# A feed-forward network's gate and up products, 17 of 22 blocks by one level of Strassen's algorithm

## Chip, core and metric

One core of a Trainium2 chip runs one program. The metric is the device time of one execution in microseconds (us), here the median of several runs. TensorE (PE in the profile) multiplies, VectorE (DVE) and ScalarE (ACT) work element by element, GpSimd is POOL, and SyncE (SP) issues the transfers.

## What is computed

One residual block on 512 tokens of width 1024: a token mixer (windowed attention beside gated linear attention), a cross attention to 256 memory tokens, a SwiGLU network, a last RMS norm. The change lies in the network and in the norms at its two ends:

```python
def _rms(t, w):
    y = t * lax.rsqrt(jnp.mean(t * t, axis=-1, keepdims=True) + EPS)
    return y * w

def _swiglu(h, w_gate, w_up, w_down):
    return (jax.nn.silu(h @ w_gate) * (h @ w_up)) @ w_down

x += _swiglu(_rms(x, w_ffn), w_gate, w_up, w_down)   # 1024 -> 2816 -> 1024
out = _rms(x, w_out)
```

## The kernel before

Tokens lie along the free axis, so a tile holds 128 features by 512 tokens; the residual stream is 8 such tiles, `res`. Every float32 product is made of three: an operand x is split by `split` (L97, L98) into a rounded high part on ACT (`H`, `ah`, `xh`) and a low part x - high on DVE (`L`, `al`, `xl`), and `prod3` gives high x high, high x low and low x high. `unit` loads a tile of weights (512 KB, by SP's queue) and splits it; its tags R, H and L have three buffers each. `block` runs the matmuls of one output tile, three for each 128 rows of the inner dimension, into a bank of PSUM. `ps_mm` has four banks that are used in turn, `ps_s` some others, `ps_t` one.

The network is the last part. `weighted` makes `zh`, `zl`, the two parts of the stream times the norm's weight; the factor of each token (1/rms, `n2.b`, spread over all partitions) is applied later. A loop over the 22 tiles of the hidden layer then runs a gate pass and an up pass of 24 matmuls 128x512 each, and behind them a chain per tile: L1022 gate times `n2.b` (DVE), SiLU (ACT, L93), L1024 times up, L1025 times `n2.b` (DVE), and a split into `ah[j]`, `al_[j]` that are kept for all 22 tiles. The squares, the sums and the reciprocal root of that norm (`Norm.add`, `Norm.finish`, `rsqrt` of nine small DVE operations) run beside the first passes. Calling the passes in order p0 (gate of tile 0), p1 (up of tile 0), p2 and so on, pass p4 writes the bank of p0.

Then come the down products: for each of 8 output tiles 66 matmuls 128x512 and one addition to `res` (L1040). The last output is made in two halves of the tokens, 66 matmuls 128x256 each. After each half the last norm is finished (L199 squares, sums on PE with a matrix of ones into `ps_t`, L216 to L178 on DVE, a spread over the partitions on PE with the identity into the same `ps_t`, L228), and `res` times this factor goes out: L1052 and L1058 on DVE, reading the spread from PSUM, L1056 on POOL, L1060 the transfer.

The order of an engine's instructions is set by a scheduler from the order of the code and a table of durations; the changed kernel writes parts of it out by hand.

Of the kernel before, what the change touches and what calls it, by code (L numbers as in the profile page):

```python
# [32 lines left out]


def build(tc, a, out):
    nc = tc.nc
    ctx = ExitStack()

    def pool(name, bufs=1, side=None, space=None):
        kw = {"name": name, "bufs": bufs, "reuse_waits": "tile"}  # L40
        if side is not None:
            kw["side"] = side
        if space is not None:
            kw["space"] = space
# [30 lines left out]
    def t2k(bufs=3):  # L75
        return tp.tile([P, 512], F32, tag="t2k", bufs=bufs, name=uniq("t2k"))
# [4 lines left out]
    def f(ap):  # L81
        return ap.bitcast(F32)
# [97 lines left out]
    class Norm:  # L180
# [23 lines left out]
            else:  # L204
                nc.vector.tensor_tensor(out=acc, in0=acc, in1=sq, op=ALU.add)

        def finish(self, spread=True, cols=None):
# [7 lines left out]
            v = cp.tile([P, nt], F32, name=uniq(f"v_{self.name}"))  # L215
            nc.vector.tensor_scalar(  # L216
                out=v, in0=ps[:, 0 : 2 * nt].rearrange("p (t c) -> p t c", c=2)[:, :, 0],
                scalar1=1.0 / D, scalar2=EPS, op0=ALU.mult, op1=ALU.add,
            )
# [89 lines left out]
    r0 = sp.tile([P, S], F32, tag="sm", bufs=4, name="r0")[:, 0:P]  # L309
    h0, l0 = (sp.tile([P, S], F32R, tag="q", bufs=8, name=n)[:, 0:P] for n in ("h0", "l0"))  # L310
# [16 lines left out]
    for u in range(1, KC // 2):  # L327
# [24 lines left out]
    wf_w = small("wf_w", [P, KC], a["norm_ffn_w"])  # L352
# [304 lines left out]
    for pr in range(2):  # L657
        qh, ql = [], []
        for h in (2 * pr, 2 * pr + 1):
            pq = ps_mm()  # L660
# [22 lines left out]
        for t in range(NT):  # L683
            kh = gp.tile([P, 2, 256], F32R, tag="kh", bufs=2, name=uniq("kh"))
            kl = kls[t % 2]
            for c in range(2):
# [26 lines left out]
            for e in range(2):  # L713
                ts = slice(t * P, (t + 1) * P)
# [295 lines left out]
    ah = [fp.tile([P, S], F32R, name=f"ah{j}") for j in range(NF)]  # L1010
    al_ = [fp.tile([P, S], F32R, name=f"al{j}") for j in range(NF)]
    for j in range(NF):
        pg = ps_mm()
        block(pg, [(unit(a["w_fg"][j]), KC)], zh, zl)
        pu = ps_mm()
        block(pu, [(unit(a["w_fu"][j]), KC)], zh, zl)
        if j == 0:
            for i in range(KC):
                n2.add(res[i])
            n2.finish()  # L1020
        t = t2k()
        nc.vector.tensor_tensor(out=t, in0=pg, in1=n2.b, op=ALU.mult)  # L1022
        table_act(t, t, AF.Silu)
        nc.vector.tensor_tensor(out=t, in0=t, in1=pu, op=ALU.mult)  # L1024
        nc.vector.tensor_tensor(out=t, in0=t, in1=n2.b, op=ALU.mult)  # L1025
        split(ah[j], al_[j], t)

    n3 = Norm("n3", S)
    for j in range(KC):
        units = []  # L1030
        for k0 in range(0, NF, KC):
            nk_ = min(KC, NF - k0)
            units.append((unit(a["w_fd"][j][:, k0 * P : (k0 + nk_) * P]), nk_))
# [100 lines left out]
```

## Time and profile before

| | |
|---|---|
| median of 3 runs | 918.81 us (918.31 to 920.23) |
| the profiled execution: own time, and its span | 919.91 us, 918.1 us |
| mean granted TensorE clock | 0.995 of full speed |
| PE / PE weight load / DVE / ACT / POOL busy | 98 / 81 / 61 / 46 / 1% |
| matmuls | 4318 |
| the network's loop and down products | about 546 to 906 us of the span |
| from the last matmul 128x256 to the span's end | 905.87 to 918.1 us |

The span is what the hardware profiler saw between the first and the last instruction; the own time of the same execution has some 1.8 us around it. A share of busy time is an average over all stages; what bounds a stage is read from what its engines wait for. Matmuls overlap, so their pace is the distance between two starts, not the listed length.

### The profile page before, as it was taken

What the parts mean: (1) busy time and instruction counts of PE and PEld (TensorE: products, weight loads), DVE (VectorE), ACT (ScalarE), POOL (GpSimd) and SP (SyncE); (2) the same over time, 40 slices, a digit from 0 to 9 for tenths busy, and PEclk for the clock granted to TensorE, in tenths of its full rate; (3) what the DMA queues carried; (4) which work ended last, traced back from release to release, by engine and by line L of the source; (5) the groups of instructions that cost most, each with busy time, mean ns of one, the idle gap of its engine ahead of it and who ended that gap; (6) DMA issues with size and microseconds to landing.
All of it is one profiled execution on the core that took longest, in us unless ns stands there. A gap on an engine that the chain in (4) does not pass through costs nothing.

```text
span 918.1 us, 11424 instructions
## 1 busy us (share of the span) xinstructions
PE 901.2 (98%) x4318; PEld 746.7 (81%) x4318; DVE 557.4 (61%) x1104; ACT 426.5 (46%) x760; POOL 7.0 (1%) x30
## 2 busy tenths in 40 slices
PE   8999999999999999999999999999999999999995
PEld 6898888887888787778888778888888888888885
DVE  6777888777343959966766996444444444323323
ACT  7576574556333838463445864223332233222220
POOL 1000000000000000000000000000000000000001
PEclk9999999999999999999999999999999999999998
DMA  7232221222232031425432222232222322323212
GB/s 249 92 115 70 69 70 69 70 69 69 92 96 89 23 115 48 143 86 161 114 115 92 70 89 95 94 107 99 92 92 92 106 100 86 104 86 103 87 41 92
DMA packets 29415, 86.11 MB, mean 94 GB/s; under 512 B 4048, under 2 KB 7760, under 8 KB 29360
## 3 DMA queue, kind: packets, MB, share of 16 engines
q1 hardware_dynamic: 29216, 85.37, 28.9%
q8 instruction: 34, 0.56, 0.2%
q14 instruction: 21, 0.17, 0.1%
q10 hardware_dynamic: 144, 0.00, 0.0%
HBM read 83.27 MB, written 2.10 MB: 93 GB/s over the span
## 4 chain that ended last, share of the span: by engine, by line
PE 89%; DVE 6%; ACT 3%; DMA 1%; issue 1%; SPq 0%; DVEq 0%; ACTq 0%
PE mm L79 80%; PE s L79 3%; PE o L79 3%; PE t L79 1%; DVE L L98 1%; PE t L545 1%; ACT pm L93 1%; DMA R<-in_w_tg 1%; PE mm L545 1%; ACT H L97 1%; DVE sl L98 1%; DVE on L747 1%; DMA x<-in_xT 0%; PE t L758 0%; DVE st L706 0%
## 5 line engine op out<-in xcount | busy, mean ns | idle before, releaser
L97 ACT CAST H<-R 128x1024 fp32r<-128x1024 f32 (+2 forms) x155 | 156.8, 1013 | 326.1 <-PE mm L79 247.0
L98 DVE TENSOR_TENSOR L<-R,H 128x1024 fp32r<-128x1024 f32 (+2 forms) x155 | 181.8, 1174 | 93.9 <-ACT H L97 93.5
L79 PE MATMUL mm<-xl,H 128*128 128x512 f32 x592 | 232.3, 392 | 0.0
L79 PE MATMUL mm<-xh,L 128*128 128x512 f32 x592 | 232.1, 392 | 0.0
L79 PE MATMUL mm<-xh,H 128*128 128x512 f32 x592 | 230.6, 390 | 0.0
L79 PEld LDWEIGHTS mm<-xh,H 128*128 128x128 f32 x592 | 111.2, 188 | 22.5
L79 PEld LDWEIGHTS mm<-xl,H 128*128 128x128 f32 x592 | 111.2, 188 | 22.1
L79 PEld LDWEIGHTS mm<-xh,L 128*128 128x128 f32 x592 | 111.3, 188 | 21.7
L79 PE MATMUL mm<-ah,H 128*128 128x512 f32 (+1 forms) x198 | 72.5, 366 | 0.0
L79 PE MATMUL mm<-ah,L 128*128 128x512 f32 (+1 forms) x198 | 72.4, 366 | 0.0
L79 PE MATMUL mm<-al,H 128*128 128x512 f32 (+1 forms) x198 | 72.4, 365 | 0.0
L79 PE MATMUL mm<-H,xh 128*128 128x512 f32 (+1 forms) x192 | 70.3, 367 | 0.0
L79 PE MATMUL mm<-L,xh 128*128 128x512 f32 (+1 forms) x192 | 70.3, 366 | 0.0
L79 PE MATMUL mm<-H,xl 128*128 128x512 f32 (+1 forms) x192 | 70.1, 365 | 0.0
L1024 DVE TENSOR_TENSOR t2k<-t2k,mm 128x512 f32<-128x512 f32 x22 | 15.0, 687 | 68.3 <-PE mm L79 67.7
L93 ACT ACTIVATE p<-sm,nm,sc 128x256 f32<-128x256 f32 (+1 forms) x64 | 36.3, 569 | 25.4 <-DVE es L519 20.3
L1022 DVE TENSOR_TENSOR t2k<-mm,rb_n 128x512 f32<-128x512 f32 x22 | 15.1, 691 | 44.9 <-PE mm L79 43.0
L79 PEld LDWEIGHTS mm<-al,H 128*128 128x128 f32 x198 | 37.3, 189 | 6.1
L79 PEld LDWEIGHTS mm<-ah,H 128*128 128x128 f32 x198 | 37.3, 189 | 6.0
L79 PEld LDWEIGHTS mm<-ah,L 128*128 128x128 f32 x198 | 37.3, 189 | 6.0
L79 PEld LDWEIGHTS mm<-L,xh 128*128 128x128 f32 x192 | 36.1, 188 | 5.5 <-DVE L L98 0.6
L79 PEld LDWEIGHTS mm<-H,xh 128*128 128x128 f32 x192 | 36.3, 189 | 5.1 <-issue 0.2
(300 smaller groups left out, 1365.7 us busy)
## 6 DMA issues: line engine op xcount, KB each, us to landing
R<-in_w_fg SPq DMA_DIRECT2D x22, 512.0 KB, 3.2
R<-in_w_fu SPq DMA_DIRECT2D x22, 512.0 KB, 3.3
R<-in_w_gate SPq DMA_DIRECT2D x16, 512.0 KB, 3.3
R<-in_w_fd SPq DMA_DIRECT2D x16, 512.0 KB, 3.5
x<-in_xT SPq DMA_DIRECT2D x16, 256.0 KB, 3.5
R<-in_w_q SPq DMA_DIRECT2D x8, 512.0 KB, 3.5
R<-in_w_attn_o SPq DMA_DIRECT2D x8, 512.0 KB, 3.3
R<-in_w_vg SPq DMA_DIRECT2D x8, 512.0 KB, 3.3
```

Source lines behind the costliest of these rows:

```text
L79: nc.tensor.matmul(o, lhsT=lhsT, rhs=rhs, start=start, stop=stop)
L93: last_table[0] = nc.scalar.activation(*args, **kw)
L97: nc.scalar.copy(out=hi, in_=src)
L98: nc.vector.tensor_tensor(out=lo, in0=src, in1=f(hi), op=ALU.subtract)
L545: nc.tensor.transpose(out=pt[:, i * P : (i + 1) * P], in_=prs[i // 2][:, i % 2, b * P : (b + 1) * P], identity=ident)
L747: nc.vector.scalar_tensor_tensor(out=on[t][:, vs], in0=on[t][:, vs], scalar=r[:, h : h + 1], in1=glaw, op0=ALU.mult, op1=ALU.mult)
L1022: nc.vector.tensor_tensor(out=t, in0=pg, in1=n2.b, op=ALU.mult)
L1024: nc.vector.tensor_tensor(out=t, in0=t, in1=pu, op=ALU.mult)
```

## The change

17 of the 22 hidden tiles (5 to 21) get their gate and up from one level of Strassen's algorithm in the form with shared sums. The matrix of the pair (gate, up) is cut into halves of the inner dimension, the tokens into two halves, and eight block products become seven, each of 4 x 3 = 12 matmuls 128x256: 84 such matmuls instead of 48 of 128x512. The first five tiles (NPLAIN) stay plain passes, p0 to p9.

What it needs beside this:

- Sums of tokens: `sums` (one `tensor_scalar` and four `scalar_tensor_tensor` 128x256 for each of four pairs of `res` tiles, L1057 and L1055) and `splits` (L103, L104, four of 128x512 for each half), made beside the plain passes.
- Sums of weights, for each group (`weight_side`): r0 (512 KB, L1101), SA (512 KB, L1103) and r1 (256 KB, L1104) are loaded by SP. GpSimd's queue adds to SA by an accumulating transfer (L1105), which waits for SA's load. DVE makes SB (L1107, which waits for the accumulating transfer, and L1108). Each of r0, SB, SA and r1 is split (SH and SL with three buffers, DH and DL with one). SA and SB share a tag S with two buffers.
- Combining the products (`group`): copies of PSUM by ACT (L1141, L1148, L1151) and DVE operations on 128x256 (L1143, L1152, L1155, L1158, L1159).
- The up factor `n2.b` is dropped. In its place `scale_stream` multiplies `res` by the rms itself (a reciprocal 128x512 of `n2.b`, L1073, and eight products 128x512, L1075), and the last norm takes EPS times the token's mean square in place of EPS.
- Down products in five parts of the inner dimension (PARTS): those of a part are run between the groups of the next one, 15 or 12 matmuls 128x512 each, and added to `res` (L1175). Each later group has one or two of them. Only the last part, five tiles, runs behind the groups, and the last output's halves are 30 matmuls 128x256 each.
- PE's order from the groups on, and that of DVE and ACT through the plain passes (table `beside`), are written by hand.

```diff
+NPLAIN = 5
+PARTS = ((0, 5), (5, 9), (9, 13), (13, 17), (17, 22))
...
+    def weight_side(j):
...
+        nc.sync.dma_start(r0, w[:, 0:1024])
+
+        nc.sync.dma_start(sa, w[:, 512:1536].rearrange("p (e c) -> p e c", e=2))
+        nc.sync.dma_start(r1[:, q0], w[:, 1024:1536])
+        nc.gpsimd.dma_start(sa, w[:, None, 1536:2048].broadcast_to([P, 2, 512]), accum_op=ALU.add)
+        h0, l0 = pair_of(r0)
+        nc.vector.tensor_tensor(out=sb[:, 0], in0=sa[:, 1], in1=r0[:, q1], op=ALU.add)
+        nc.vector.scalar_tensor_tensor(
+            out=sb[:, 1], in0=sb[:, 0], scalar=-1.0, in1=r0[:, q0], op0=ALU.mult, op1=ALU.subtract
+        )
+        hb, lb = pair_of(sb.rearrange("p e c -> p (e c)"))
+        ha, la = pair_of(sa.rearrange("p e c -> p (e c)"))
...
+        return {
+            "r11": (h0[:, q1], l0[:, q1]), "r21": (h0[:, q0], l0[:, q0]), "t2": (hb[:, q0], lb[:, q0]),
+            "t1": (ha[:, q1], la[:, q1]), "t3": (ha[:, q0], la[:, q0]), "t4": (hd, ld), "r22": (hb[:, q1], lb[:, q1]),
+        }
...
+    def group(j):
...
+        product(pa, w, "r11", True)
+        nc.scalar.copy(out=g[:, t0], in_=pa)
+        product(pb, w, "r21", True)
+        nc.vector.tensor_tensor(out=g[:, t0], in0=pb, in1=g[:, t0], op=ALU.add)
+        yield
...
+        product(pa, w, "t2", False)
+        nc.scalar.copy(out=g[:, t1], in_=pa)
+        product(pc, w, "t1", True)
+        product(pa, w, "t3", False)
+        nc.scalar.copy(out=s3, in_=pa)
+        nc.vector.tensor_tensor(out=s3, in0=pc, in1=s3, op=ALU.subtract)
+        yield
+        product(pc, w, "r22", False)
+        nc.vector.tensor_tensor(out=g[:, t1], in0=g[:, t1], in1=pc, op=ALU.subtract)
+        activation(g, j)
+        product(pa, w, "t4", False)
...
+    beside = {
+        0: [lambda: squares(range(4))],
+        1: [lambda: squares(range(4, 8)), norm_2],
+        2: [lambda: sums(0), lambda: plain_act(0)],
+        3: [lambda: splits(0)],
+        4: [lambda: plain_act(1), lambda: sums(1)],
+        5: [lambda: splits(1)],
+        6: [lambda: plain_act(2), lambda: scale_stream(range(2))],
+        7: [lambda: scale_stream(range(2, KC))],
+        8: [lambda: plain_act(3), lambda: first_weights.append(weight_side(NPLAIN))],
+        9: [],
+    }
...
+                g = group(j)
+                next(g)
+                if two == 2 and not late:
+                    down(p - 1, next(at))
+                next(g)
+                down(p - 1, next(at))
+                next(g)
+                if two == 2 and late:
+                    down(p - 1, next(at))
```

**The order on DVE after the norm's factor.** DVE of the kernel before, behind `rsqrt`, where `rb_n` is the spread factor, `mm` a bank of PSUM (`mm_5457` is p0's) and `L` the low half of a tile of weights:

```order
L98 TENSOR_TENSOR L_5676<-R_5674,H_5675 128x1024
L175 SCALAR_TENSOR_TENSOR nwy_5549<-nwt_5550,nwy_5549 128x4
L176 SCALAR_TENSOR_TENSOR nwt_5550<-nwy_5549 128x4
L177 TENSOR_TENSOR nwt_5550<-nwt_5550,v_n_1050_5546 128x4
L178 SCALAR_TENSOR_TENSOR rt_n_1051_5548<-nwt_5550,nwy_5549 128x4
L1022 TENSOR_TENSOR t2k_5566<-mm_5457,rb_n_1055_5564 128x512
```

The same place of the changed kernel, where `zx` are the sums of tokens and `mm_5447` is p0's bank:

```order
L181 SCALAR_TENSOR_TENSOR rt_n_1057_5532<-nwt_5534,nwy_5533 128x4
L1190 TENSOR_SCALAR alr<-v_n_1056_5530 128x4
L101 TENSOR_TENSOR L_5553<-R_5551,H_5552 128x1024
L1057 TENSOR_SCALAR zx_5582<-x_0_4470,wf_w 128x256
L1055 SCALAR_TENSOR_TENSOR zx_5582<-x_0_4470,wf_w,zx_5582 128x256
L1055 SCALAR_TENSOR_TENSOR zx_5583<-x_4_4632,wf_w,zx_5582 128x256 x2
L1055 SCALAR_TENSOR_TENSOR zx_5584<-x_4_4632,wf_w,zx_5583 128x256
L1057 TENSOR_SCALAR zx_5582<-x_1_4509,wf_w 128x256
L1055 SCALAR_TENSOR_TENSOR zx_5582<-x_1_4509,wf_w,zx_5582 128x256
L1055 SCALAR_TENSOR_TENSOR zx_5583<-x_5_4673,wf_w,zx_5582 128x256 x2
L1055 SCALAR_TENSOR_TENSOR zx_5584<-x_5_4673,wf_w,zx_5583 128x256
L1179 TENSOR_TENSOR t2k_5595<-mm_5447,rb_n_1061_5548 128x512
```

The operation that empties p0's bank (L1022 before, L1179 now) has moved behind ten sums.

**The order on ACT at the first group.** ACT of the changed kernel from the last plain tile on. SH_5849, SH_5855, SH_5859 and DH_5863 are the first group's weights, SH_6058 is the second group's r0, H_6028 and H_6106 are weights of down products, and the copies read the first group's bank `pa`:

```order
L100 CAST SH_5849<-R_5841 128x1024
L100 CAST H_6028<-R_6027 128x640
L100 CAST SH_5855<-SB_5844 128x1024
L100 CAST SH_5859<-SA_5843 128x1024
L100 CAST DH_5863<-R_5842 128x512
L100 CAST SH_6058<-R_6050 128x1024
L1141 COPY t2k_5904<-mm_5902 128x256
L96 ACTIVATE t2k_5892<-t2k_5892 128x512
L100 CAST H_6106<-R_6105 128x640
L100 CAST a_5896<-t2k_5892 128x512
L1148 COPY t2k_5904<-mm_5902 128x256
L1151 COPY s_1120_5932<-mm_5902 128x256
```

The copies L1141 and L1148, for which PE waits before t2 and t3 accumulate further in `pa`, stand behind casts of weights that are still to come.

**The order on DVE in a later lap, with the semaphores that each waits for.** DVE of the changed kernel from one group's SB to the next group's middle. 6401 is the next group's SB, `mm_6285` and `mm_6349` are two down products, and `s_6302` is the running group's `pc`:

```order
L1107 TENSOR_TENSOR SB_6401<-SA_6400,R_6398 128x512 [waits DMAHW2_49,DMASW3_49]
L101 TENSOR_TENSOR SL_6407<-R_6398,SH_6406 128x1024 [waits Activation_49]
L1108 SCALAR_TENSOR_TENSOR SB_6401<-SB_6401,R_6398 128x512 [waits DVE_49]
L101 TENSOR_TENSOR L_6455<-R_6453,H_6454 128x640 [waits DMAHW5_49,Activation_49]
L1175 TENSOR_TENSOR x_4_4632<-x_4_4632,mm_6285 128x512 [waits PE_49]
L101 TENSOR_TENSOR L_6519<-R_6517,H_6518 128x640 [waits DMAHW6_49,Activation_49]
L101 TENSOR_TENSOR SL_6413<-SB_6401,SH_6412 128x1024 [waits PE_49,Activation_49]
L1152 TENSOR_TENSOR s_1176_6303<-s_6302,s_1176_6303 128x256 [waits Activation_49]
```

New in such a lap are the wait of L1107 for the accumulating transfer (DMASW3) and all that stands in line behind it.

## Rows read from the trace of the kernel before

**Rows 1.** The page: busy time, share of the span and instructions of each engine.

```profile
PE 901.2 (98%) x4318; PEld 746.7 (81%) x4318; DVE 557.4 (61%) x1104; ACT 426.5 (46%) x760; POOL 7.0 (1%) x30
```

**Rows 2.** Windows: busy PE, PEld, DVE, ACT, POOL; clock, DMA share, GB/s.

```profile
566.00:886.00 320.00, 320.00 (x1414) 265.05 (x1413) 134.42 (x158) 95.78 (x117) 0.00 (x0) 1.00 0.29 94
```

**Rows 3.** Timeline of PE, last output: start, length, engine, line, operation.

```profile
879.83 0.39 PE L79 MATMUL mm<-al,H 128*128 128x512 f32 x1
...
888.22 0.39 PE L79 MATMUL mm<-ah,L 128*128 128x512 f32 x1
...
888.56 0.28 PE L79 MATMUL mm<-al,H 128*128 128x256 f32 x1
...
890.60 0.28 PE L79 MATMUL mm<-ah,H 128*128 128x256 f32 x1
```

**Rows 4.** Timeline of DVE at the network's start; in brackets idle time before and releaser.

```profile
571.77 0.69 DVE L1022 TENSOR_TENSOR t2k<-mm,rb_n 128x512 f32<-128x512 f32 x1 [0.81 <-PE mm L79]
```

**Rows 5.** Timeline of ACT at the same place.

```profile
563.56 0.59 ACT L228 COPY rb_n<-t 128x512 f32<-128x512 f32 x1 [4.50 <-PE t L79]
```

**Rows 6.** Groups of DVE by form: count | busy, mean ns of one | idle before.

```profile
L98 DVE TENSOR_TENSOR L<-R,H 128x1024 fp32r<-128x1024 f32 x136 | 166.1, 1222 | 89.1 <-ACT H L97 88.7
L98 DVE TENSOR_TENSOR al<-t2k,ah 128x512 fp32r<-128x512 f32 x22 | 15.0, 684 | 0.7 <-ACT ah L97 0.7
...
L539 DVE TENSOR_SCALAR p<-p,dn 128x256 f32<-128x256 f32 x48 | 13.7, 350 | 0.4
L706 DVE SCALAR_TENSOR_TENSOR st<-st,aend,s 128x256 f32<-128x256 f32 x28 | 12.9, 477 | 0.4
L101 DVE SCALAR_TENSOR_TENSOR xl<-x,wf_w,xh 128x512 fp32r<-128x512 f32 x8 | 6.0, 750 | 0.0
...
L536 DVE RECIPROCAL dn<-dn 128x4 f32<-128x4 f32 x16 | 2.9, 178 | 0.5
...
L898 DVE RECIPROCAL dn<-dn 128x2 f32<-128x2 f32 x8 | 1.3, 163 | 0.4 <-ACT pm L93 0.3
...
L1040 DVE TENSOR_TENSOR x<-x,mm 128x256 f32<-128x256 f32 x2 | 0.8, 420 | 8.3 <-PE mm L79 8.3
```

**Rows 7.** Groups of ACT by form, the same columns.

```profile
L97 ACT CAST H<-R 128x1024 fp32r<-128x1024 f32 x136 | 142.8, 1052 | 295.2 <-PE mm L79 223.3 <-issue 71.6
L97 ACT CAST ah<-t2k 128x512 fp32r<-128x512 f32 x22 | 13.7, 623 | 14.4 <-DVE t2k L1025 14.4
...
L228 ACT COPY rb_n<-t 128x256 f32<-128x256 f32 x2 | 0.7, 372 | 7.6 <-PE t L79 7.6
```

**Rows 8.** DMA issues: count, size, median us from issue to landing.

```profile
R<-in_w_fg SPq DMA_DIRECT2D x22, 512.0 KB, 3.2
...
R<-in_w_fd SPq DMA_DIRECT2D x8, 384.0 KB, 3.1
```

**Rows 9.** Timeline of all engines, the two halves of the last output.

```profile
896.56 0.42 DVE L1040 TENSOR_TENSOR x<-x,mm 128x256 f32<-128x256 f32 x1 [5.71 <-PE mm L79]
...
900.31 0.68 PE L79 MATMUL t<-ident,rt_n 128*128 128x128 f32 x4
...
902.83 0.75 DVE L1058 TENSOR_TENSOR fin<-x,t 128x256 f32<-128x256 f32 x2
...
906.19 0.42 DVE L1040 TENSOR_TENSOR x<-x,mm 128x256 f32<-128x256 f32 x1 [2.61 <-PE mm L79]
...
907.17 0.38 PE L79 MATMUL t<-ones,sq 128*128 128x2 f32 x2 [0.90 <-ACT sq L199]
...
908.04 0.16 DVE L216 TENSOR_SCALAR v_n<-t 128x2 f32<-128x2 f32 x1 [1.43 <-PE t L79]
...
909.92 1.19 PE L79 MATMUL t<-ident,rt_n 128*128 128x128 f32 x4 [1.92 <-DVE rt_n L178]
```

**Rows 10.** Windows behind the last product, columns as in Rows 2.

```profile
908.00:910.00 2.00, 0.08 (x1) 0.11 (x1) 1.46 (x9) 0.00 (x0) 0.00 (x0) 0.82 0.00 0
910.00:912.00 2.00, 1.11 (x4) 0.81 (x4) 0.45 (x2) 0.37 (x1) 0.40 (x1) 0.50 0.00 0
```

More of the change, by code (lines that the diff above doesn't have):

```diff
@@ L47, in build @@
     cp = ctx.enter_context(pool("cp"))
-    edge = ctx.enter_context(pool("ep", side="right")).tile([P, 24], F32, name="edge")
+    ep_ctx = pool("ep", side="right")
+    edge = ep_ctx.__enter__().tile([P, 24], F32, name="edge")
     wp = ctx.enter_context(pool("wp"))
@@ L214, in finish @@
                 terms(ps[:, 2 * t : 2 * t + 2], [(x[:, t * P : (t + 1) * P], ones[:, 0:2]) for x in parts])
[L215 to L219, printed above, removed]
+            v = self.v = cp.tile([P, nt], F32, name=uniq(f"v_{self.name}"))
+            sums = ps[:, 0 : 2 * nt].rearrange("p (t c) -> p t c", c=2)[:, :, 0]
+            if eps is None:
+                nc.vector.tensor_scalar(out=v, in0=sums, scalar1=1.0 / D, scalar2=EPS, op0=ALU.mult, op1=ALU.add)
+            else:
+                nc.vector.scalar_tensor_tensor(
+                    out=v, in0=sums, scalar=1.0 / D, in1=eps[:, cs.start // P : cs.stop // P], op0=ALU.mult, op1=ALU.add
+                )
             self.tok = cp.tile([P, nt], F32, name=uniq(f"rt_{self.name}"))
@@ L1005, in build @@
     mep_ctx.__exit__(None, None, None)
+    ep_ctx.__exit__(None, None, None)
+    HS = S // 2
+    t0, t1 = slice(0, HS), slice(HS, S)
     fp_ctx = pool("fp")
     fp = fp_ctx.__enter__()
[L1010 to L1020, printed above, removed]
+    fe_ctx = pool("fe", side="right")
@@ new lines, in build, with act_tile, hidden, sums @@
+    fedge = fe_ctx.__enter__().tile([P, 8], F32, name="fedge")
+    nc.gpsimd.memset(fedge, 0.0)
+    fw_ctx = pool("fw", side="right")
+    fw = fw_ctx.__enter__()
+    act = {}
+    def act_tile(n):
+        return fp.tile([P, 2, S], F32R, tag="a", bufs=9, name=uniq(n))
+    def hidden(j, t):
+        act[j] = act_tile("a")
+        split(act[j][:, 0], act[j][:, 1], t)
+    zt = {o: fp.tile([P, 4, 2, HS], F32R, name=f"z_{o}") for o in ("t1", "t2", "t3", "t4")}
+    token_sums = {}
+    def sums(i):
+        tiles = [act_tile("zx") for _ in range(3)]
+        x12, x1, x2, x3, x4 = [f(x)[:, e].rearrange("p (k c) -> p k c", k=2) for x in tiles for e in range(2)][:5]
+        for e in range(2):
+            k, q = 2 * i + e, 4 + 2 * i + e
+            wa, wb = wf_w[:, k : k + 1], wf_w[:, q : q + 1]
+            def stt(o, x, w, y, op):
+                nc.vector.scalar_tensor_tensor(out=o[:, e], in0=x, scalar=w, in1=y[:, e], op0=ALU.mult, op1=op)
+            nc.vector.tensor_scalar_mul(x12[:, e], res[k][:, t1], wa)
+            stt(x1, res[k][:, t0], wa, x12, ALU.subtract)
+            stt(x2, res[q][:, t1], wb, x1, ALU.add)
+            stt(x3, res[q][:, t1], wb, x12, ALU.subtract)
+            stt(x4, res[q][:, t0], wb, x2, ALU.subtract)
+        token_sums[i] = x1, x2, x3, x4
@@ new lines, in splits, with scale_stream @@
+    def splits(i):
+        x1, x2, x3, x4 = token_sums[i]
+        for o, x, sign in (("t2", x2, -1.0), ("t1", x1, -1.0), ("t3", x3, None), ("t4", x4, -1.0)):
+            split(zt[o][:, 2 * i : 2 * i + 2, 0], zt[o][:, 2 * i : 2 * i + 2, 1], x, sign)
+    rms = cp.tile([P, S], F32, tag="rb", bufs=2, name="rms")
+    def scale_stream(js):
+        if js[0] == 0:
+            nc.vector.reciprocal(rms, n2.b)
+        for i in js:
+            nc.vector.tensor_tensor(out=res[i], in0=res[i], in1=rms, op=ALU.mult)
@@ new lines, in product, with activation @@
+    def product(o, w, op, first):
+        h, lo = w[op]
+        for k in range(4):
+            ks = slice(k * P, (k + 1) * P)
+            for i, (l_, r_) in enumerate(prod3(h[:, ks], lo[:, ks], *token_parts(op, k))):
+                nc.tensor.matmul(
+                    o, lhsT=l_, rhs=r_, start=first and k == 0 and i == 0, stop=k == 3 and i == 2,
+                    skip_group_check=not first,
+                )
+    def activation(g, j):
+        nc.vector.tensor_tensor(out=g, in0=g, in1=n2.b, op=ALU.mult)
+        table_act(g, g, AF.Silu)
@@ new lines, in group @@
+    def group(j):
+        w = first_weights.pop() if first_weights else weight_side(j)
+        pa, pb = ps_mm()[:, :HS], ps_mm()[:, :HS]
+        g = t2k()
+        product(pa, w, "r11", True)
[3 more added lines that the diff above has]
+        yield
+        pc = ps_s()[:, :HS]
+        s3 = tp.tile([P, S], F32, tag="sq", bufs=1, name=uniq("s3"))[:, t0]
+        product(pa, w, "t2", False)
[9 more added lines that the diff above has]
+        product(pa, w, "t4", False)
+        nc.vector.scalar_tensor_tensor(out=g[:, t0], in0=pa, scalar=-1.0, in1=g[:, t0], op0=ALU.mult, op1=ALU.mult)
+        nc.vector.tensor_tensor(out=g[:, t1], in0=s3, in1=g[:, t1], op=ALU.mult)
+        hidden(j, g)
+        yield
@@ new lines, in down_units, with down_block, down, plain_act @@
+    def down_units(p, i):
+        lo, hi = PARTS[p]
+        return [(unit(a["w_fd"][i][:, lo * P : hi * P]), hi - lo)]
+    def down_block(o, p, units, cs):
+        ks = range(*PARTS[p])
+        block(o, units, [act[k][:, 0, cs] for k in ks], [act[k][:, 1, cs] for k in ks])
+    def down(p, i):
+        units = down_units(p, i)
+        pd = ps_mm()
+        down_block(pd, p, units, slice(0, S))
+        nc.vector.tensor_tensor(out=res[i], in0=res[i], in1=pd, op=ALU.add)
+    def plain_act(j):
@@ L1021, in build, with squares @@
         t = t2k()
-        nc.vector.tensor_tensor(out=t, in0=pg, in1=n2.b, op=ALU.mult)
+        nc.vector.tensor_tensor(out=t, in0=outs[2 * j], in1=n2.b, op=ALU.mult)
         table_act(t, t, AF.Silu)
-        nc.vector.tensor_tensor(out=t, in0=t, in1=pu, op=ALU.mult)
-        nc.vector.tensor_tensor(out=t, in0=t, in1=n2.b, op=ALU.mult)
-        split(ah[j], al_[j], t)
+        nc.vector.tensor_tensor(out=t, in0=t, in1=outs[2 * j + 1], op=ALU.mult)
+        hidden(j, t)
+    def squares(js):
+        for i in js:
+            n2.add(res[i])
@@ new lines, in build @@
+    plain = [a[n][j] for j in range(NPLAIN) for n in ("w_fg", "w_fu")]
+    us = [unit(x) for x in plain[:2]]
+    outs = []
+    with tc.manual_schedule(engines={mybir.EngineType.DVE, mybir.EngineType.Activation}):
+        for i in range(2 * NPLAIN):
+            if i + 2 < 2 * NPLAIN:
+                us.append(unit(plain[i + 2]))
+            outs.append(ps_mm())
+            block(outs[i], [(us[i], KC)], zh, zl)
+            for do in beside[i]:
+                do()
+        plain_act(NPLAIN - 1)
@@ new lines, in build @@
+    with tc.manual_schedule(engines={mybir.EngineType.PE}):
+        for p in range(1, len(PARTS)):
+            js = list(range(*PARTS[p]))
+            n = [KC // len(js)] * len(js)
+            for i in (-1, 0, 1, 2, 3)[: KC - sum(n)]:
+                n[i] += 1
+            at = iter(range(KC))
+            for j, two in zip(js, n):
+                late = j in (js[0], NF - 1)
+                g = group(j)
[7 more added lines that the diff above has]
+                    down(p - 1, next(at))
@@ L1028, in build @@
     n3 = Norm("n3", S)
     for j in range(KC):
[L1030 to L1033, printed above, removed]
+        units = down_units(len(PARTS) - 1, j)
         W = S if j < KC - 1 else S // 2
@@ L1121 @@
     }
+    w_fg, w_fu = arrays["w_fg"], arrays["w_fu"]
+    arrays["w_fgu"] = np.concatenate(
+        [w[NPLAIN:, :, c] for w in (w_fg, w_fu) for c in (slice(512, 1024), slice(0, 512))], 2
+    )
+    arrays["w_fg"], arrays["w_fu"] = w_fg[:NPLAIN], w_fu[:NPLAIN]
     nc = bacc.Bacc("TRN2", target_bir_lowering=False, num_devices=1)
```

33 lines of the change are left out of this document (30 added, 3 removed).

## The prediction

> **What bounds the kernel now.** I read the page first: PE is busy 98% of the span [rows 1]. The windows then say whether that holds where the change lies: over 320 us of the network PE is busy for all 320 at full clock, while DVE has work for 134 of them, ACT for 96, and the DMA engines for 29% [rows 2]. So PE's matmuls are the bound there, and every matmul taken out is worth its pace as long as nothing makes PE wait. The pace is read off the timeline: 38 matmuls 128x512 start between 879.83 and 888.22, 37 distances of 0.2268 us; 18 of 128x256 between 888.56 and 890.60, 17 distances of 0.1200 [rows 3]. A half-width matmul thus costs 53% of a whole one, not half.
>
> The profiled execution took 919.9 us by its own clock, 1.1 above the median of the runs, 918.8. I work out differences in the trace and add them to the median; they are too small for the 0.1% between the two to matter.
>
> **(a) The products.** A group has 84 x 0.1200 = 10.08 us where gate and up had 48 x 0.2268 = 10.89. That is 0.81 less, and for 17 groups **-13.7**. Seven products in place of eight would be one eighth, 23 us; the narrower matmuls give back two fifths.
>
> **(b) The last output.** 132 narrow matmuls (15.84) become 51 wide and 30 narrow (11.57 + 3.60 = 15.17): **-0.7**. The other down products are the same matmuls in another order.
>
> These are the only gains. All else is a question of what PE waits for.
>
> **(c) The way into the first group.** Here the order on DVE decides. Passes take 24 x 0.2268 = 5.44. Before, L1022 at 571.77 waited for the end of p4 [rows 4], so p4 began at about 566.3.
>
> - p4 needs p0's bank, which now L1179 empties, behind ten sums. The factor is spread at 563.6 + 0.6 [rows 5]; an L of 1.2 that stood inside the root's chain is now behind it, so I put the factor at 563.0. Then come the cast 1.05 [rows 7], the L 1.22, eight `scalar_tensor_tensor` at 0.477 and two `tensor_scalar` at 0.350 (4.4 with a little overlap), L1179 0.69 [rows 6]: 570.4. PE waits **4.1**.
> - From 570.4 DVE has some 30 us of work (31 less overlaps) in line until p9's low weights: two activations with their splits at 3.3, the first one's rest 2.6, five L at 1.22, eight splits of sums (5.9), ten more sums (4.4), two scalings (1.4) and a reciprocal 128x512 [rows 6]. No row shows that reciprocal. Widths 2 and 4 take 163 and 178 ns [rows 6], 7.5 ns a column, so 163 + 510 x 7.5 = 4.0 us by extension; the other end is 0.69, as for any operation of that shape. I take 4.0, since its own kind is the nearer row. p9's L ends at 600.4, and PE, five passes behind 570.4, needs it at 598.0: **2.4**.
> - The first group's r0 is split behind six scalings, an activation and its split (scalings 3.7, L1179 0.69, SiLU, an L, L1181, the casts of a and of SH0, SL0): 609.5, against p9's end at 605.4. r11 waits **3.4** in all.
> - t2 waits for ACT's copy of `pa`, which stands behind the cast of the second group's r0. That load waits for a buffer that L1108 gives back at about 611.2; 3.2 for the load [rows 8], 1.05 cast, 0.37 copy [rows 7] make 615.9, and PE is there at 611.9: **4.0**.
> - t3 waits for its copy in the same way, behind a load that waits for DL: about **1.0**.
>
> The sum is 14.9; I take **+14**, as consecutive operations overlap by some hundredths. Bounds: 8.3 (cheap reciprocal, sums at 0.35 each; p9's and r11's waits gone) and 14.9.
>
> **(d) The tail.** Before, the second half's products hid the first half's norm: from L1040 at 896.56 to the last of its DVE outputs at 902.83 + 0.75 are 7.0 us, and the second half's L1040 came at 906.19 [rows 9]. Now the halves are 3.6 apart. The second half's sums must go into the one `ps_t` bank that those outputs read, so they start 7.0 + 0.4 (L1250 of the second half now falls inside the chain) - 3.6 = 3.8 behind its L1250; 0.87 later is v, at 4.7 in place of 908.04 - 906.19 = 1.85. That is 2.8 later; the spread at half clock adds 0.5 (0.68 against 1.19) [rows 9]. Some of it overlaps, and I take **+3**, bounds 2 and 3.9.
>
> **(e) The laps of the groups.** DVE has about 12 us in a group of 15.5 with two down products (10.08 + 2 x 2.72) and 10.7 in one of 12.8, so it is not full, but its line is serial. From the end of t3 of one group the chain is: cast SHb 1.05, SLb 1.22 (gives back the S buffer), SA's load 3.2, the accumulating transfer T, L1107 0.68, SL0 1.22, L1108 0.75 (gives back an R buffer), on SP's queue behind SA the down weights 3.1, their cast 0.62, SHb 1.05, SLb 1.22, L1152 0.42 [rows 6, 7, 8]: 14.5 + T. It must be through when r22 of the next group wants `pc`, a lap and one down product later: 15.5 + 2.7 = 18.2. So T up to 3.7, or 3.9 with the overlaps, is hidden. With one down product the chain lacks the load and its cast (10.8 + T against 15.5): T up to 4.7. Four laps are of the first kind and five of the second; the others have more room, by a third down product or by down products of 15 matmuls.
>
> T has no row. It cannot well be shorter than a plain load of as many bytes, 3.2 [rows 8]; if what it adds to has to be read first in full, it is twice that, 6.4. Nothing is nearer to either end, so I take 4.8: 4 x 0.9 + 5 x 0.1 = **+4.1**. At 6.4 it is 4 x 2.5 + 5 x 1.7 = 18.5.
>
> **Costed at nothing:** the additions to `res` for the parts and the five fewer `n2.b` products (DVE's spare 22%), the loads (a quarter more bytes for a group; the engines are at 29% [rows 2]). If DVE's cover went, 0.69 a down product would show.
>
> Sum: -13.7 - 0.7 + 14 + 3 + 4.1 = +6.7, so **925.5 us**.
>
> **Rivals.**
>
> - *Cheap preparation (faster).* If the reciprocal costs 0.7 and the sums 0.35, DVE's line into the first group is 6 us shorter, p9 and r11 don't wait, and (c) is 8.3; with T under 3.9 the total is -14.4 + 8.3 + 3 = -3.1: 915.7. For it: two widths are a thin base for 7.5 ns a column. Against: the sums are strided over two tiles and depend on each other. It decides where (c) plus (d) falls below 12.5.
> - *A short accumulation.* T near 3.2: no lap waits, 918.8 + 2.6 = 921.4. For it: the plain load's row. Against: it reads two operands.
> - *A long one.* T at 6.4: 925.5 + 14.4 = 939.9, and DVE at L1107 would head the waits.
> - *The clock.* In the tail PE's granted clock fell from 1.00 to 0.82 and 0.50 once it had stood still from 908.0 to 909.9 [rows 9, 10], that is to 1.2 GHz. The waits before p4 and t2 are twice as long. If one of them is followed by a pass at half pace, that is 5.4 more: 931. Against: no row shows the level behind a wait inside a stretch at 98%.
>
> The Trainium skill, page "DMA: Bandwidth & Descriptors", section "Anatomy of one DMA — SWDGE (gpsimd) path", fits a transfer of GpSimd's queue as a fixed 2.0 us plus its bytes at 436 GB/s; an estimate from that is 3.2 us for 512 KB, which would be the short accumulation, 921.4. No row before shows a transfer of that queue, and the plain load's 3.2 agrees with the same figure on another queue.
>
> The Trainium skill, page "TensorE: Matmul & The Clock Gate", section "HAM oscillation — how this bites in real kernels", says that a matmul kernel that waits for data again and again restarts at the lower clock each time; that would be the clock's rival, 931. The tail's two windows agree with the fall itself.
>
> **How the numbers follow.** Chances: the forecast as worked (T between 4 and 5.6) 0.32; cheap preparation 0.25; a short accumulation 0.20; a long one 0.13; the clock 0.10. The number is that of the likeliest, 925.5; its own range, by the bounds of (c) and (d) and T up to 5.6 (4 x 1.7 + 5 x 0.9 = 11.3), is 919 to 934. The low end, 911, is the cheap preparation with the copies' waits at t2 and t3 gone too (-14.4 + 4 + 3 = -7.4); the high end, 943, the long accumulation with (c) and (d) at their upper bounds (939.9 + 0.9 + 0.9 = 941.7) and little more. A measurement of this kernel can tell 0.2%, 1.8 us, from no change. Faster than 917.0: 0.25, the cheap preparation. Within: 0.12, the upper edge of that case and the lower of the short accumulation, from 917 to 920.6. Slower: 0.63.
>
> **What would show it.** PE's first long wait before p4 with L1179 as releaser, then one before p9 for an L, before r11 for SL0, before t2 with ACT's L1141; L1073's length (4.0 or 0.7); the landing time of L1105's transfer, and DVE's wait at L1107; ACT's chain in front of r22 in the four laps; v of the second half 4.7 behind its L1250; the granted clock in the stretches behind p4's and t2's waits. I am wrong if PE runs through p4 and t2 without a gap, or if the groups keep to 15.5 and 12.8 us a lap while the time is above 922.

## The result and the profile after

The changed kernel takes 984.6 us (median of 4, 980.3 to 986.5) where the kernel before takes 919.3: a ratio of 1.070 (95% interval 1.067 to 1.074), 65 us more. The forecast was 925.5, its range ended at 943. The sign was right, the size far off.

The page of the changed kernel, busy time and DMA issues (the latter: count, size, median us from issue to landing):

```profile
span 984.7 us, 13017 instructions
...
PE 912.4 (93%) x4879; PEld 777.9 (79%) x4879; DVE 656.0 (67%) x1304; ACT 476.6 (48%) x869; POOL 27.6 (3%) x48
...
L1107 DVE TENSOR_TENSOR SB<-SA,R 128x512 f32<-128x512 f32 x17 | 11.8, 691 | 63.2 <-DMA SA<-in_w_fgu 63.2
...
SA<-in_w_fgu SPq DMA_DIRECT2D x17, 512.0 KB, 4.2
SA<-in_w_fgu POOLq DMA_DIRECT2D x17, 512.0 KB, 6.7
R<-in_w_fgu SPq DMA_DIRECT2D x17, 512.0 KB, 3.9
```

PE fell from 98 to 93% of a longer span [rows 1], so it is no longer the bound. DVE stood 63 us before L1107, in 16 of 17 cases for the accumulating transfer, which takes 6.7 us from issue to landing, twice the plain load of [rows 8].

Waits of the changed kernel (us in total, times, longest):

```profile
PE s L1126 <- DVE s L1152: 32.1, 12, 4.1
...
PE mm L1126 <- ACT t2k L1148: 12.7, 5, 4.3
...
PE mm L82 <- DVE t2k L1179: 3.9, 1, 3.9
...
PE mm L1126 <- ACT SH L100: 2.9, 1, 2.9
...
PE mm L1126 <- ACT t2k L1141: 1.4, 1, 1.4
```

The first two are PE in the groups, waiting for DVE's L1152 (which stands behind the low part of SB) and for ACT's copies: 45 us, of which 2.9 (a first wait of each row, 1.6 and 1.3) fall in the first group. The others belong to the way into that group.

One lap in the chain of work that ended last (start, length, what):

```profile
648.53 1.23 DVE SL L101
649.79 3.89 DMA SA<-in_w_fgu
654.25 6.60 DMA SA<-in_w_fgu
663.37 2.91 DMA R<-in_w_fd
668.02 1.22 DVE SL L101
```

This is the chain of part (e) of the prediction: the low part of SB, SA's load, the accumulation, SB, the down weights' load, and again a low part of SB. It comes round in 668.02 - 648.53 = 19.5 us, where PE has work for 10.08 + 2 x 3.40 = 16.9. In a lap with one down product PE has 12.8, and there too the chain is longer: from 901.51 to 917.96 are 16.5.

### The profile page after: what moved, and what is told of

The parts are those of the page before. It is cut to its first block, busy times and chain, and to the rows that moved or that the text cites. A ratio compares the mean times of both kernels' runs of the same rounds, so it can differ in the third digit from the quotient of the medians.

```text
span 984.7 us, 13017 instructions
## 1 busy us (share of the span) xinstructions
PE 912.4 (93%) x4879; PEld 777.9 (79%) x4879; DVE 656.0 (67%) x1304; ACT 476.6 (48%) x869; POOL 27.6 (3%) x48
## 4 chain that ended last, share of the span: by engine, by line
PE 60%; DMA 16%; DVE 15%; ACT 5%; issue 3%; SPq 0%; DVEq 0%; ACTq 0%; POOLq 0%
PE mm L82 45%; DMA SA<-in_w_fgu 12%; DMA R<-in_w_fd 4%; PE mm L1126 3%; PE o L82 3%; DVE SL L101 3%; PE s L82 3%; PE s L1126 3%; ACT SH L100 2%; DVE L L101 2%; PE t L82 1%; DVE SB L1107 1%; DVE SB L1108 1%; PE t L551 1%; DVE zx L1055 1%
## 5 line engine op out<-in xcount | busy, mean ns | idle before, releaser
L100 ACT CAST H<-R 128x1024 fp32r<-128x1024 f32 (+4 forms) x137 | 123.8, 905 | 226.4 <-PE mm L82 117.1
L101 DVE TENSOR_TENSOR L<-R,H 128x1024 fp32r<-128x1024 f32 (+4 forms) x137 | 142.5, 1041 | 57.5 <-ACT H L100 56.9
L82 PE MATMUL mm<-xh,H 128*128 128x512 f32 x320 | 125.3, 393 | 3.9 <-DVE t2k L1179 3.9
L82 PE MATMUL mm<-xl,H 128*128 128x512 f32 x320 | 126.9, 397 | 0.0
L82 PE MATMUL mm<-xh,L 128*128 128x512 f32 x320 | 126.7, 397 | 0.0
L82 PE MATMUL mm<-a,H 128*128 128x512 f32 (+1 forms) x362 | 112.7, 393 | 0.0
L82 PEld LDWEIGHTS mm<-a,H 128*128 128x128 f32 x362 | 67.4, 194 | 11.9
L82 PE MATMUL mm<-a,L 128*128 128x512 f32 (+1 forms) x181 | 70.3, 388 | 0.0
L82 PEld LDWEIGHTS mm<-xh,L 128*128 128x128 f32 x320 | 60.5, 189 | 11.1 <-DVE L L101 0.2
L1126 PE MATMUL mm<-z_t,SH 128*128 128x256 f32 x272 | 52.2, 291 | 14.2 <-ACT t2k L1148 12.7
L1126 PEld LDWEIGHTS mm<-z_t,SH 128*128 128x128 f32 x272 | 43.9, 197 | 16.9 <-ACT t2k L1148 14.4
L1107 DVE TENSOR_TENSOR SB<-SA,R 128x512 f32<-128x512 f32 x17 | 11.8, 691 | 63.2 <-DMA SA<-in_w_fgu 63.2
```

The lines of the kernel that those rows point to most:

```text
L82: nc.tensor.matmul(o, lhsT=lhsT, rhs=rhs, start=start, stop=stop)
L1107: nc.vector.tensor_tensor(out=sb[:, 0], in0=sa[:, 1], in1=r0[:, q1], op=ALU.add)
L1126: nc.tensor.matmul(o, lhsT=l_, rhs=r_, start=first and k == 0 and i == 0, stop=k == 3 and i == 2, skip_group_check=not first,)
```

## Experiments

A time without an interval is that of a single run. The four runs of e2 lie 4 us apart and the ten of e8 7 us, so differences of 1 or 2 us between single runs are read from the traces and not from the times.

**Does the accumulating transfer cost the 65 us, and by what?** Theory A: it lies in a chain that every lap must go through. B: it slows the other transfers. C: DVE and ACT have too much in line.

*e1_no_sum*, the transfer left out:

```diff
-        nc.gpsimd.dma_start(sa, w[:, None, 1536:2048].broadcast_to([P, 2, 512]), accum_op=ALU.add)
```

> The accumulating transfer is left out, so SA lacks the low half of up (that part of the computation is missing). Theory A, the lap chain (low part of SB, SA's load, accumulating transfer, SB, down weights' load, back to the low part of the next SB): without 6.7 us of transfer a lap's chain is about 13 us against 15.5 of PE, so the 60 us that the groups lost come back: about 925 us, and PE's wait for DVE's L1152 (32 us) is gone. Rival B, contention (GpSimd's queue slows SP's loads from 3.2 to 4.2): also about 925, and SA's plain load lands in 3.2. Rival C, DVE and ACT have too much in line for a group: over 960.

924.1 us, as A and B said (SA's load lands in 3.6, where B had 3.2). C falls: DVE, ACT and PE do the same work. The windows say where the time was, the changed kernel first, then e1 (columns as in [rows 2]):

```profile
640.00:930.00 290.00, 247.96 (x1608) 227.83 (x1607) 164.19 (x251) 104.03 (x163) 16.82 (x14) 0.92 0.47 119
```

```profile
640.00:870.00 230.00, 229.72 (x1625) 212.80 (x1624) 159.77 (x247) 104.42 (x162) 0.00 (x0) 1.00 0.36 114
```

About as many matmuls took 290 us and 230. Of the 60 us PE was idle for 42; the other 18 are matmuls that took longer, at a granted clock of 0.92 in the mean where e1 has 1.00.

*e2_three_S*, the chain cut by a buffer, with the transfer kept:

```diff
-        sa = fw.tile([P, 2, 512], F32, tag="S", bufs=2, name=uniq("SA"))
-        sb = fw.tile([P, 2, 512], F32, tag="S", bufs=2, name=uniq("SB"))
+        sa = fw.tile([P, 2, 512], F32, tag="S", bufs=3, name=uniq("SA"))
+        sb = fw.tile([P, 2, 512], F32, tag="S", bufs=3, name=uniq("SB"))
```

and nine buffers of hidden tiles made eight.

> A third buffer for SA and SB (one of the nine buffers of hidden tiles given up for the room). The same bytes, transfers and operations; SA's load and its accumulation no longer wait for the low part of SB of the group before. A: the chain is cut, about 925 us, with the accumulating transfer still at 6 to 7 us. B: contention is the same, so over 960, and loads still land in 4 us. C: over 960.

950.6 us (ratio 1.035, 1.033 to 1.037): 34 of the 60 us, between A and B. Its DMA issues and its chain:

```profile
SA<-in_w_fgu POOLq DMA_DIRECT2D x17, 512.0 KB, 8.0
R<-in_w_fgu SPq DMA_DIRECT2D x17, 512.0 KB, 6.5
```

```profile
648.76 3.77 DMA R<-in_w_fd
654.17 6.45 DMA R<-in_w_fgu
666.25 3.61 DMA R<-in_w_fd
671.25 6.72 DMA R<-in_w_fgu
```

The accumulation has left the chain. But now it runs at the same time as r0's load, which takes 6.5 us in place of 3.9, and the loads through the R buffers make a new chain, round in 17.5 us.

*e11_three_S_copy* is e2, instruction for instruction, but the transfer overwrites:

```diff
-        nc.gpsimd.dma_start(sa, w[:, None, 1536:2048].broadcast_to([P, 2, 512]), accum_op=ALU.add)
+        nc.gpsimd.dma_start(sa, w[:, None, 1536:2048].broadcast_to([P, 2, 512]))
```

> e2_three_S, instruction for instruction in the same order, except that the transfer of GpSimd's queue overwrites SA and does not add to it (the sums with the low half of up are missing). If what kept e2 at 950 is the adding (8 us itself, and r0's load beside it at 6.5): the transfer lands in about 5 us as in e6, r0's load in 4 to 5, and the time is 924 to 932. If it is e2's order or its buffers (a chain through R that is too long even so): 945 to 950.

924.8 us. So what kept e2 at 950 is the adding, not its order, its buffers or the bytes written: without it the same transfer and r0's load land in (DMA issues from 640 to 870 us)

```profile
SA<-in_w_fgu POOLq DMA_DIRECT2D x13, 512.0 KB, 5.5
R<-in_w_fgu SPq DMA_DIRECT2D x13, 512.0 KB, 5.2
```

*e5_idle_sum_beside* and *e6_idle_copy_beside* put the transfer, adding or copying, into a tile that nothing reads (GpSimd first reads two elements of SA, so that it starts when it did; the tile is zeroed once ahead of the network and takes the room of one of the nine buffers of hidden tiles):

```diff
+        nc.gpsimd.tensor_copy(out=scr[:, 0, 0:2], in_=sa[:, 0, 0:2])
+        nc.gpsimd.dma_start(scr, w[:, None, 1536:2048].broadcast_to([P, 2, 512]), accum_op=ALU.add)
-        nc.gpsimd.dma_start(sa, w[:, None, 1536:2048].broadcast_to([P, 2, 512]), accum_op=ALU.add)
```

> The accumulating transfer of the same bytes, started at the same moment (when SA has landed), but into a tile that nothing reads; SA lacks the low half of up, as in e1_no_sum (that part of the computation is missing). So the chain is cut whole and only what the transfer does to others is left. The chain alone costs (A): 924, as e1. Contention costs too (B, as the r0 loads of 6.5 us in e2_three_S hint): r0's load again near 6.5 us and 935 to 950.

> As e5, but the transfer of GpSimd's queue only writes its tile and does not add to it (the sum is missing as in e5). If the adding is what is slow and in the way: it lands in 3 to 4 us, r0's load stays at 4, about 925 us. If it is the queue or the bytes: 6 to 8 us and the time of e5.

933.3 and 925.2 us against e1's 924.1. The idle sum costs 9 us against e1 and 8 against e6, from which it differs by the adding alone: this is contention, just under the range expected. It is not r0's load that pays for most of it (3.6 in the median). PE waits for ACT's copy L1151, which stands each time behind a cast of down weights that ACT had to wait for. The idle copy's 1 us is less than single runs can tell. The transfers, then those waits, e5 first:

```profile
scr<-in_w_fgu POOLq DMA_DIRECT2D x17, 512.0 KB, 7.3
```

```profile
scr<-in_w_fgu POOLq DMA_DIRECT2D x17, 512.0 KB, 4.9
```

```profile
PE mm L1129 <- ACT t2k L1151: 5.4, 7, 2.0
```

```profile
PE mm L1129 <- ACT t2k L1151: 1.3, 2, 0.7
```

*e3_halves* makes the transfer two of 256 KB, first the half that L1107 reads:

```diff
-        nc.gpsimd.dma_start(sa, w[:, None, 1536:2048].broadcast_to([P, 2, 512]), accum_op=ALU.add)
+        for e in (1, 0):
+            nc.gpsimd.dma_start(sa[:, e], w[:, 1536:2048], accum_op=ALU.add)
```

> The accumulating transfer of 512 KB as two of 256 KB, that for the half that L1107 reads first. A with a price that grows with bytes (2 us fixed, the rest with size): L1107's transfer lands in about 4.4, 2.3 less a lap, some 35 us less: about 950 us. A with a fixed price: 6 us each, no gain, about 985. B or C: about 985.

956.8 us, 28 less than the change: near A with a price that grows with bytes. The first of the two lands in 4.3 us in the median of the trace, as that price had it (4.4).

*e4_sum_on_DVE* makes the sum on DVE:

```diff
-        nc.sync.dma_start(r1[:, q0], w[:, 1024:1536])
-        nc.gpsimd.dma_start(sa, w[:, None, 1536:2048].broadcast_to([P, 2, 512]), accum_op=ALU.add)
+        nc.sync.dma_start(r1, w[:, 1024:2048])
+        nc.vector.tensor_tensor(out=sa, in0=sa, in1=r1[:, None, q1].broadcast_to([P, 2, 512]), op=ALU.add)
```

> The accumulating transfer is replaced by one DVE addition 128x1024 (1.22 us), its operand loaded by SP (512 KB in place of 256 for r1). A: T is 1.2 in place of 6.7 and the chain fits in a lap: 925 to 935 us, the upper end if DVE, at 13.3 of 15.5 us and 11.9 of 12.8, now makes PE wait. B: about 925 to 935 too. C: DVE has more in line, so as slow as the change or slower, 985 or more.

925.7 us, with the computation complete: 59 of the 65 us gained by one edit, although DVE is now busy for 17 us more (673.4 against 656.0). C falls once more.

**What is left against the kernel before.** e4 still takes 6.4 us more than before, so the 14 us of matmuls saved are spent elsewhere.

*e7_activation_first* is e4 with `2: [lambda: plain_act(0), lambda: sums(0)]` in the table.

> e4_sum_on_DVE, with the first activation (L1179) ahead of the ten sums of tokens. If each wait on the way into the first group stands alone: p4's 3.9 us are gained, 921.8. If DVE's line as a whole is the bound there: p4's wait goes, but p9 or r11 waits that much longer, 925 to 926.

925.05 us: DVE's line as a whole is the bound there. p4's wait of 3.9 is gone, and PE waits 4.3 for low weights of the later passes in its place.

*e8_light_DVE* shortens that line:

```diff
-            nc.vector.reciprocal(rms, n2.b)
+            pb = ps_t()
+            for t in range(NT):
+                nc.tensor.matmul(pb[:, t * P : (t + 1) * P], lhsT=root[:, t : t + 1].broadcast_to([P, P]), rhs=ident, start=True, stop=True)
+            nc.scalar.copy(out=rms, in_=pb)
...
-            nc.vector.tensor_tensor(out=res[i], in0=res[i], in1=rms, op=ALU.mult)
+            nc.gpsimd.tensor_tensor(out=res[i], in0=res[i], in1=rms, op=ALU.mult)
```

and the second half of the last norm takes the bank `ps_o`.

> e7, with the rms made from 128x4 and spread by PE in place of the reciprocal 128x512 (3.4 us), the eight scalings of res on GpSimd in place of DVE (5 us), and the second half of the last norm in another PSUM bank. If DVE's line is the bound into the first group: 8 us less there and the waits before p4, p9 and r11 (7.3 us, and the low clock behind them, 2) go; the tail gains some 3: 911 to 915 us, faster than before (919.3). If the tail's delay is not the bank's: 915 to 918.

923.7 us (ratio to before 1.0047, 1.0030 to 1.0063), a miss by 9. The second bank did help: from the last matmul 128x256 to the end are 15.2 us, in e7 17.0. The timelines of POOL, DVE and PE in e8 show what went wrong:

```profile
591.47 13.91 POOL L1079 TENSOR_TENSOR x<-x,rms 128x512 f32<-128x512 f32 x8 [365.17 <-ACT rms L1077]
```

```profile
587.04 1.22 DVE L101 TENSOR_TENSOR L<-R,H 128x1024 fp32r<-128x1024 f32 x1
...
598.00 2.31 DVE L1109 TENSOR_TENSOR SA<-SA,R 128x1024 f32<-128x1024 f32 x1
600.23 2.30 DVE L101 TENSOR_TENSOR SL<-R,SH 128x1024 fp32r<-128x1024 f32 x1
602.46 1.77 DVE L1111 TENSOR_TENSOR SB<-SA,R 128x512 f32<-128x512 f32 x1
...
607.77 1.23 DVE L101 TENSOR_TENSOR SL<-SB,SH 128x1024 fp32r<-128x1024 f32 x1 [1.11 <-ACT SH L100]
```

```profile
612.10 0.79 PE L1130 MATMUL mm<-z_t,SH 128*128 128x256 f32 x2 [6.72 <-ACT t2k L1145]
```

While GpSimd multiplies (591.5 to 605.4), DVE's subtraction 128x1024 takes 2.30 us, before and after 1.22. DVE is late with the operations that give back the buffer of the second group's r0, ACT's copy stands behind the cast of that r0, and PE waits 6.7 us before t2.

*e9_scale_in_groups* scales on DVE, in `down`, next to the first additions:

```diff
+        if p == 0:
+            nc.vector.tensor_tensor(out=res[i], in0=res[i], in1=rms, op=ALU.mult)
         nc.vector.tensor_tensor(out=res[i], in0=res[i], in1=pd, op=ALU.add)
```

> e7_activation_first with the rms spread by PE (no reciprocal 128x512) and the scalings of res on DVE beside the first group and not on GpSimd; the tail as in the change. If GpSimd's products beside DVE's are what made DVE's operations twice as long in e8_light_DVE (2.3 us in place of 1.2): none is over 1.3 now, the first group begins about 6 us earlier, 918 to 921, although the tail is again the slower one. If DVE slowed for another reason: 924.

921.4 us, at the expected range's edge, although the tail is again that of the change. No operation of DVE 128x1024 is over 1.23 us in the mean now, and PE's wait before t2 is 3.8 in place of 6.7.

*e10_all* adds the order of the last outputs and one order on ACT:

```diff
+    halves = [(j, c0, S // 2) for c0 in (0, S // 2) for j in (KC - 2, KC - 1)]
+    for j, c0, W in [(j, 0, S) for j in range(KC - 2)] + halves:
...
+            with tc.issue_after(after.ins):
+                nc.scalar.copy(out=h, in_=src)
```

(`after` is the copy L1141 of the group before, `h` the high part of r0.)

> e9 with two more edits: the last two outputs in halves (so 7.2 us of products lie behind the first half's norm, as before 7.9) and the cast of the next group's r0 held behind the first copy of pa. If the tail's 4.9 us are the price of the short halves and t2's wait (about 4) that of the order on ACT: 911 to 914, faster than the kernel before (919.1). If the tail stays: 915 to 917.

916.2 us, 0.9965 of the kernel before (0.9953 to 0.9977): faster than both kernels by measurement, by 0.35%, though 2 us short of what was expected. The two edits weren't tried apart. In the traces the wait before t2 is 2.1 (3.8 in e9), and the tail is shorter, but not that of the kernel before. The timeline of the second half, the changed kernel first, then e10:

```profile
967.85 0.42 DVE L1250 TENSOR_TENSOR x<-x,mm 128x256 f32<-128x256 f32 x1
...
972.67 0.56 PE L82 MATMUL t<-ones,acc_n 128*128 128x2 f32 x2 [2.73 <-DVE fin L1268]
...
974.55 0.16 DVE L223 SCALAR_TENSOR_TENSOR v_n<-t,alr 128x2 f32<-128x2 f32 x1 [2.02 <-PE t L82]
```

```profile
899.28 0.28 PE L82 MATMUL mm<-a,L 128*128 128x256 f32 x1
...
899.93 1.74 DVE L1280 TENSOR_TENSOR fin<-x,t 128x256 f32<-128x256 f32 x5
901.58 0.42 DVE L1262 TENSOR_TENSOR x<-x,mm 128x256 f32<-128x256 f32 x1
...
903.37 0.16 DVE L223 SCALAR_TENSOR_TENSOR v_n<-t,alr 128x2 f32<-128x2 f32 x1 [1.37 <-PE t L82]
```

From the addition to v are 6.7 us in the change, 1.8 in e10, and 1.85 before [rows 9]. But in e10 the addition itself comes late: the products end at 899.6, and DVE first makes the outputs of the first half (L1280). From the last matmul 128x256 to the span's end are 12.3 us before, 17.1 in the change and 14.1 in e10: 3.0 of the 4.9 us came back, and the 1.9 left are about what e10 falls short by.

*e12_all_three_S* is e10 with e2's buffers.

> e10_all (916.2) with e2's third S buffer and eight buffers of hidden tiles. If the last waits in the groups (ACT's copies and loads that come late, some 3 us) are due to SA's late load: 912 to 915. If not, or if the missing buffer of hidden tiles costs as much: 915 to 918.

918.2 us (ratio to before 0.999, 0.998 to 1.000), no better than e10: once nothing accumulates, a third S buffer is worth nothing, or no more than the hidden tile given up for it. The two were not tried apart.

## Why the prediction was wrong

Point by point, by its own steps:

**(a), (b) held, and a little more.** In e1's windows PE is busy for 229.7 of 230 us at full clock. Two matmuls of PE's timeline in e1, 47 distances apart, show a pace in the groups of 0.118 where [rows 3] have 0.120:

```profile
661.96 0.28 PE L1125 MATMUL s<-xh,SH 128*128 128x256 f32 x1
...
667.50 0.28 PE L1125 MATMUL mm<-xh,SL 128*128 128x256 f32 x1
```

For 17 x 84 matmuls that is 3 us more than the -14.4.

**(c) held in its sum, 13.7 in place of 14, partly by luck.** p4 waited 3.9 (forecast 4.1) with L1179 as releaser, r11 2.9 for the cast and 0.5 for the low part (3.4), t3 1.3 (1.0). p9 did not wait (2.4): the reciprocal took 0.7 less than the extension from [rows 6] gave, and PE came 1.5 later for the clock (below). t2 waited 1.4 (4.0), since the second group's r0 landed earlier than forecast:

```profile
L1073 DVE RECIPROCAL rms<-rb_n 128x512 f32<-128x512 f32 x1 | 3.3, 3345 | 0.0
```

The waits are 10.0 together. What made up the sum was the clock, which (c) had left out. Behind p4's wait the granted clock is 0.52 from 569 to 572 us, the lower level, 1.2 GHz. Two matmuls of PE's timeline, 5 distances of 0.428 us apart where [rows 3] have 0.2268:

```profile
569.55 0.63 PE L82 MATMUL mm<-xl,H 128*128 128x512 f32 x1
...
571.69 0.49 PE L82 MATMUL mm<-xh,H 128*128 128x512 f32 x1
```

p4 took 6.89 us in place of 5.44, 1.5 more. Behind r11's wait the matmuls of r11 and r21 went at little more than half the pace (granted clock 0.51 from 607 to 613), two of them with 20 distances of 0.213 us between them:

```profile
607.83 0.41 PE L1126 MATMUL mm<-xh,SH 128*128 128x256 f32 x1
...
612.10 0.41 PE L1126 MATMUL mm<-xh,SL 128*128 128x256 f32 x1
```

For the 24 matmuls of the two products that is 2.2 us. So the clock's rival came true here, but for 3.7 us and not 5.4, and beside the forecast rather than in its place. e7 adds what the sum of single waits did not say: they are one bound, DVE's line, and a wait taken away alone comes back at the next place.

**(d) was 4.9, not 3.** v came 6.7 behind the addition, not 4.7: the halves are 967.85 - 965.14 = 2.7 apart and not 3.6, and the four sums on PE took 1.9 us, at half clock (0.50), and not 0.87. The 0.5 added for the spread was nothing: in the second half it takes 1.19 now and took 1.19 before [rows 9].

**(e) is the step that failed: 60 in place of 4.** The chain was named link by link, and e1, e2 and e4 show that it is the right one. Three things were wrong in its price. First, T: I took 4.8 between 3.2 and 6.4, and it is 6.7; the upper bound, twice the plain load, was no bound. Second, SA's load was put at 3.2 as in [rows 8] and takes 4.2 (the down weights' load took 2.9 in the lap shown, forecast 3.1). With these two alone the same sum would give 4 x 3.8 + 5 x 3.0 = 30. Third, for the other half: I asked whether the chain is through when the next r22 wants `pc`, charged nine laps of sixteen and said that the others "have more room". But the chain closes on itself. Its links from SA's load to the next low part of SB, as I had them, are 11.8 + T; with 6.7 for T and 4.2 for SA's load they are the 19.5 us of the lap shown. Each lap takes as long as the longer of chain and PE, and what one lap is late the next does not make up. From r22 to r22 all sixteen laps were longer than in e1, by 0.7 to 7.2 us, 3.9 on average; in the first three parts four laps take 80 to 82 us, whether PE needs 66 for them, as e1 shows for the first part, or 61 and 62, as for the next two. That includes 18 us of low clock, which I had only as a rival and at 5 us.

One term was put at nothing: what the transfers do to each other. In the changed kernel a load of down weights (256 or 320 KB) takes 5.6 us in the median where it runs beside the accumulation for over 1 us (16 loads), and 2.7 where it doesn't meet it (13). The median of all with 256 KB is 4.3, in e1 2.6 (lines below, e1 second). e5 and e6 put a price of 8 us on the adding where nothing waits for it; how much of the 60 is contention in the changed kernel itself stays open.

```profile
R<-in_w_fd SPq DMA_DIRECT2D x24, 256.0 KB, 4.3
```

```profile
R<-in_w_fd SPq DMA_DIRECT2D x24, 256.0 KB, 2.6
```

The steps add up to -17.4 + 13.7 + 4.9 + 60.5 = 61.7, against 65.3 measured; 3.6 us are not placed. The rival "a long one" had the mechanism and its place (DVE at L1107 heads the waits), with 939.9 as its time: the second and third of these faults.

Two figures of the prediction do not follow from its own terms, and nothing above hangs on them: the times for r11, 609.5 and 605.4, are 4.1 apart and not 3.4, and the lower bounds of (c) and (d) give 915, not 919, as the low end of the forecast's own range.

"A short accumulation" and the page behind it fall: the Trainium skill, page "DMA: Bandwidth & Descriptors", section "Anatomy of one DMA — SWDGE (gpsimd) path", leads by its fit to an estimate of 3.2 us for 512 KB; here such a transfer took 4.9 to 5.5 when it only copied and 6.7 to 8.0 when it added, with loads of SP's queue beside it, and the measurement decides.

The Trainium skill, page "TensorE: Matmul & The Clock Gate", section "HAM oscillation — how this bites in real kernels", speaks of kernels that wait again and again and pay for it in clock; this trace agrees, with 0.92 against 1.00 and 18 us.

## What to carry to other kernels

A chain that runs through a buffer's reuse closes on itself once per lap: add up its links round the loop and compare the sum with the lap, and if it is longer, charge the difference for every lap and not only once. An accumulating transfer is no free addition: price it at its own landing time plus what it does to the loads beside it, and put it where neither lies in a chain; one DVE addition of 1.2 us was 59 us cheaper here. And where work is spread over more, shorter pieces, look at what the longer pieces had hidden, such as a norm behind half an output.

## What the runs showed of the hardware

- An accumulating transfer of 512 KB on GpSimd's queue lands in 6.7 to 8.0 us (medians of the runs), the same transfer without the adding in 4.9 to 5.5, a plain load of 512 KB on SP's queue in 3.2 to 4.4 where no transfer of GpSimd's queue runs. Its harm to others is mutual: where it meets r0's load, both are slow (8.0 and 6.5, in e2).
- GpSimd's products of two SBUF tiles lengthen DVE's operations on two SBUF tiles (128x1024 up to 2.31 against 1.22 us, in e8); one with an operand in PSUM kept its 0.69 us beside them (L1185 at 595.17). The eight products took GpSimd 13.9 us, where DVE needs some 5, and moving them there gained nothing here. The Trainium skill, page "SBUF — State Buffer", section "Who interferes with whom", says that a DVE instruction with two SBUF inputs contends with a GpSimd instruction that reads SBUF; the trace agrees, with those numbers.
- A reciprocal on DVE costs by its width: 0.163 and 0.178 us for 2 and 4 columns [rows 6], 3.35 us for 128x512, where a product of that shape takes 0.69.
